# Seven block products instead of eight in parts of a gated MLP's matrix products, with the up product held the other way round

## The chip, the cores and the metric

The kernel runs on one core of one Trainium2 chip. The metric is the device time in microseconds (us) of one execution; the number given is the median of several runs. Everything is computed in float32. TensorE takes the big products in the form fp32r, so each float32 factor is cut into a rounded high part and a remainder, and a product is the sum of three: high x high, high x low and low x high.

## The reference

A trunk of two layers works on 256 tokens of width 2048. Each layer normalises, mixes the tokens (first an mLSTM, then an HGRN2 recurrence), adds the result, normalises again and runs a gated MLP with a convolution of width 3 over the tokens:

```python
def conv_glu(hn, w_up, conv_w, conv_b, w_down):
    u = hn @ w_up                       # 2048 -> 2 x 5504
    a, v = jnp.split(u, 2, axis=-1)
    ...
    for j in range(CONV_W):
        c = c + ap[:, j:j + s] * conv_w[j]
    return (jax.nn.gelu(c, approximate=False) * v) @ w_down   # 5504 -> 2048
...
    h = h + mix
    h = h + conv_glu(rmsnorm(h, norm_ffn_g[layer]), ...)
return rmsnorm(h, final_g)
```

The change is in `conv_glu` alone, in both layers.

## The kernel before

**Stream of chunks.** The program is one list of chunks that `stream` (L152) works through; each chunk is a product of all 256 tokens with a strip of weights. The strip's 16 to 22 k-tiles (128 rows of the contraction each) come from memory in pieces. `split_weights` (L122) is the generator of these pieces: a DMA on SyncE's queue brings up to 2048 columns to a tile `raw` (3 buffers), and for each 1024 of them ScalarE casts the high part `wh` (L147) and VectorE subtracts it to get the low part `wl` (L148); `wh` and `wl` have 4 buffers each. `stream` keeps 3 pieces ahead of the one that is multiplied (LOOK).

**Two forms of product.** In a chunk of kind "fm" the weights stand still in TensorE and the tokens move (L202, L209): 512 columns (high and low part of 256 tokens) pass the high weights, then 256 columns pass the low weights. The result has features on the partitions and tokens along the row. In a chunk of kind "tm" the tokens stand still and 512 columns of weights move, three matmuls for each half of the tokens (L192 to L194); the result has tokens on the partitions.

**The gated MLP** (`ffn`, L809). Its 43 feature tiles are worked through in two parts, 22 and 21. For each tile of a part there is one "fm" chunk over 16 k-tiles, with the tile's columns of a and of v as its two products. `done_up` (L820) sums the two halves of each (`fm_scaled`), multiplies by the norm's factor, applies the convolution along the row (L829 to L831), gelu and the gate, and cuts the result into high and low part: the tile `g`. Then four "tm" chunks (`project`) multiply the part's `g` tiles with 512 columns of the down weights each and add to the residual `hm` (L378).

**PSUM** has 8 banks: 4 for the chunks' sums, of which a chunk takes 2, and 4 for everything else (`aux`).

**Side work.** Small jobs (a norm's transposes, the mixers' heads) are generators in `Side`; `stream` calls `side.tick` with the modelled microseconds of each matmul, and a job whose time has come emits its next instructions. `side.until` forces jobs on until something exists, `side.drain` until none is left. On top of the order in which the program emits them, the compiler's planner orders instructions within each engine by its own estimate of when they are ready. At run time each engine takes its instructions in that order.

**Norms.** A norm's `add(c)` (L260) runs as soon as columns 512c to 512c + 511 of the residual are complete; it squares them and starts `turn` (L269), which transposes the residual's tiles (`pz`, L276) into the tiles `xt`, high and low part, for the next stage.

Of the kernel before, what the change touches and what calls it, by code (L numbers as in the profile page):

```python
# [8 lines left out]
F32 = mybir.dt.float32  # L9
# [11 lines left out]
FA = 22  # L21
FB = FT - FA
# [33 lines left out]
def trunk_kernel(ctx, tc, xT, x_d, fg_d, pp_d, cst_d, w_first, w_aq, w_ak, w_av, w_ao, w_aout,  # L56
                 w_bq, w_bv, w_bg, w_bout, w_up, w_down, out, mscr):
# [6 lines left out]
    psm = ctx.enter_context(tc.tile_pool(name="psm", bufs=4, space=PSUM))  # L64
    psa = ctx.enter_context(tc.tile_pool(name="psa", bufs=4, space=PSUM))
# [14 lines left out]

    def aux(name):
        return psa.tile([P, 512], F32, tag="aux", name=name)


    class Side:
# [3 lines left out]
        def push(self, gen):  # L89
            self.jobs.append([gen, self.now])  # L90
# [19 lines left out]
        def drain(self):  # L110
            self.until(lambda: not self.jobs)
# [9 lines left out]

    def split_weights(chunks):  # L122

        first = True
        for ch in chunks:
            total = ch.nk * ch.width
# [24 lines left out]

    def stream(chunks):  # L152
# [10 lines left out]
        for ch in chunks:  # L163
            if ch.before:
                ch.before()
            ps = [psm.tile([P, 512], F32, tag="mm", name="mm") for _ in range(3 if ch.kind == "first" else 2)]
# [49 lines left out]

    def fm_sum(ps, dst):
# [15 lines left out]
    class Norm:  # L233

        def __init__(self, gname, goff):
            self.g, self.o = gname, goff
            self.xs, self.done = [None] * KT, False

# [21 lines left out]
        def add(self, c):  # L260

            if c == 0:
                self.ss = ev.tile([P, 2, 4], F32, tag="ss8", bufs=2, name="ss8")
            cs = slice(512 * c, 512 * c + 512)
            for t in range(2):
                square(hm[:, t, cs], self.ss[:, t, c:c + 1])
            side.push(self.turn(c))

        def turn(self, c):  # L269
            yield 2.5  # L270
            for k0 in (4 * c, 4 * c + 2):
# [5 lines left out]
                for k in (k0, k0 + 1):  # L277
                    self.take(k, pz[:, (k - k0) * T:(k - k0 + 1) * T])
# [32 lines left out]
        def x(self, k):  # L311
            side.until(lambda: self.xs[k] is not None)
            return self.xs[k]

# [77 lines left out]
    def mlstm(norm, nxt):  # L392
# [204 lines left out]
        def end():  # L597
            side.drain()
            stack.close()

# [5 lines left out]
    def hgrn(norm, nxt):  # L606
# [193 lines left out]
        def end():  # L800
            side.drain()
            stack.close()

# [5 lines left out]
    def ffn(layer, norm, nxt):  # L809
        stack = ExitStack()  # L810
        box = {}
        chunks = []

        def begin():
            box["mp"] = stack.enter_context(tc.tile_pool(name="ff", bufs=1))
            box["mp"].tile([P, LEAD], F32, name="lead")
            if isinstance(nxt, FinalNorm):
                nxt.begin(box["mp"])

        def done_up(f, i, GT):  # L820
            def go(ps):
                mp, R = box["mp"], norm.R
                a = mp.tile([P, T], F32, tag="a", bufs=2, name="a")
                v = mp.tile([P, T], F32, tag="v", bufs=2, name="v")
                c = mp.tile([P, T], F32, tag="c", bufs=2, name="c")
                fm_scaled(ps[0], R, a)
                fm_scaled(ps[1], R, v)
                cw = [col("conv_w", (layer * 3 + w) * FT + f) for w in range(3)]
                dve.tensor_scalar(c, a, cw[1], col("conv_b", layer * FT + f), ALU.mult, ALU.add)  # L829
                dve.scalar_tensor_tensor(c[:, 1:T], a[:, 0:T - 1], cw[0], c[:, 1:T], ALU.mult, ALU.add)  # L830
                dve.scalar_tensor_tensor(c[:, 0:T - 1], a[:, 1:T], cw[2], c[:, 0:T - 1], ALU.mult, ALU.add)  # L831
                act.activation(c, c, AF.Gelu)
                dve.tensor_tensor(c, c, v, ALU.mult)
                g = slot(i, "g", mp)
                act.copy(g[:, 0:T], c)
                dve.tensor_tensor(g[:, T:2 * T], c, g[:, 0:T].bitcast(F32), ALU.subtract)
                GT.append(g)
            return go

        for part, (f0, nf) in enumerate(((0, FA), (FA, FB))):  # L840
            GT = []
            for i in range(nf):
                chunks.append(Chunk("fm", w_up[layer, f0 + i], KT, norm.x, done_up(f0 + i, i, GT),
                                    begin if f0 + i == 0 else None,
                                    turns=1 if part and i == 0 else 0))
            chunks += project(lambda c: w_down[layer, c][:, f0 * 512:(f0 + nf) * 512], nf,
                              lambda k, GT=GT: GT[k], nxt if part else None)
        return chunks, stack.close
# [9 lines left out]
    n0, n1, n2, n3 = Norm("mix_g", 0), Norm("ffn_g", 0), Norm("mix_g", KT), Norm("ffn_g", KT)  # L858
    nf = FinalNorm()
    chunks = mlstm(n0, n1)  # L860
    c, close0 = ffn(0, n1, n2)
    chunks += c
    c = hgrn(n2, n3)
# [7 lines left out]
    c, close1 = ffn(1, n3, nf)  # L871
    chunks += c
# [4 lines left out]
def _cols(w, width):  # L877
# [3 lines left out]
    return np.ascontiguousarray(v).reshape(N // width, P, (K // P) * width)  # L881

# [18 lines left out]
def layout(x, norm_mix_g, norm_ffn_g, mlstm_w_in, mlstm_b_gate, mlstm_head_g, mlstm_w_out, hgrn_w_in, hgrn_lb,  # L901
# [8 lines left out]
    up = A(ffn_w_up).reshape(2, KT, P, 2, FT, P).transpose(0, 4, 2, 1, 3, 5)  # L910
# [18 lines left out]
        w_up=np.ascontiguousarray(up).reshape(2, FT, P, KT * 256),  # L929
        w_down=np.stack([_cols(A(ffn_w_down)[i], 512) for i in range(2)]),  # L930
# [3 lines left out]
def build(nc, ins, out_shape=(2, P, D), **kw):  # L934
# [4 lines left out]
    with tile.TileContext(nc, schedule_with_timeline_sim=True) as tc:  # L939
        with ExitStack() as ctx:  # L940
# [3 lines left out]
                         ap["w_bout"], ap["w_up"], ap["w_down"], out, mscr, **kw)  # L944
# [12 lines left out]
```

## Time and profile before

| what | value |
|---|---|
| median of 3 runs | 2436.88 us (2436.76 to 2436.89) |
| span of the profiled execution | 2434.7 us |
| TensorE's granted clock, mean | 0.998 |
| first layer's gated MLP: up, down, up, down | 245.5, 119.7, 237.5, 117.2 us |
| second layer's: up, down, up | 245.5, 119.7, 237.5 us |
| transferred | 451.85 MB, mean 186 GB/s |

The profile shows one execution. PE is TensorE's matmuls, PEld its loads of the operand that stands still, DVE is VectorE, ACT ScalarE, POOL GpSimd. Matmuls are pipelined, so one lasts longer than the distance to the next. A group's row gives line, engine, operation, out<-in, shape and count, then after the first bar busy us and mean ns of one, and after the second bar the engine's idle time ahead of them and what ended it. Rows of a timeline give start and length in us.

### The profile page before, as it was taken

How to read it: one execution, taken by the hardware profiler on the slowest of the kernel's cores; microseconds unless marked ns; L12 is line 12 of the kernel's file. 1: busy time of each engine (PE TensorE's matmuls, PEld its weight loads, DVE VectorE, ACT ScalarE, POOL GpSimd, SP SyncE). 2: the span in 40 equal slices, each digit the busy share in tenths (PEclk: the TensorE clock that was granted, in tenths of full speed). 3: DMA queues.
4: the chain of work that ended last, by engine and by line, in shares of the span. 5: the costliest groups of instructions: out<-in, count | busy, mean ns of one | idle time of the engine just before them, and what ended most of it. 6: DMA issues, size and time to landing. Idle time of an engine off the chain costs nothing.

```text
span 2434.7 us, 36201 instructions
## 1 busy us (share of the span) xinstructions
PE 2421.4 (99%) x14319; PEld 2069.5 (85%) x14319; DVE 1691.8 (69%) x2768; ACT 1207.5 (50%) x1831; POOL 160.7 (7%) x219
## 2 busy tenths in 40 slices
PE   9999999999999999999999999999999999999998
PEld 7888888888888888888888888888888888888887
DVE  7766566777645777656888989885777754677754
ACT  6655455444434444445555555545554543444443
POOL 0100000000000000001222222220000000000000
PEclk9999999999999999999999999999999999999999
DMA  7654555555555555555445554455555555555553
GB/s 288 197 182 158 188 175 188 191 190 191 185 197 189 190 184 183 192 184 183 170 171 174 174 174 167 166 183 195 181 189 189 191 195 196 184 183 188 190 187 141
DMA packets 66202, 451.85 MB, mean 186 GB/s; under 512 B 7648, under 2 KB 8160, under 8 KB 13424
## 3 DMA queue, kind: packets, MB, share of 16 engines
q1 hardware_dynamic: 63792, 442.91, 52.6%
q0 software_dynamic: 1232, 5.31, 1.0%
q8 instruction: 112, 1.84, 0.3%
q10 hardware_dynamic: 1008, 1.32, 0.2%
q14 instruction: 58, 0.48, 0.1%
HBM read 447.35 MB, written 2.16 MB: 185 GB/s over the span
## 4 chain that ended last, share of the span: by engine, by line
PE 99%; ACT 0%; DMA 0%; issue 0%; DVE 0%; SPq 0%; POOLq 0%; POOL 0%
PE mm L202 36%; PE mm L209 18%; PE mm L192 13%; PE mm L194 13%; PE mm L193 13%; PE pn L508 1%; PE pd L694 1%; PE py L742 1%; PE pz L276 0%; PE pa L694 0%; PE S L494 0%; DMA raw<-in_w_first 0%; PE pz L763 0%; ACT xt L214 0%; PE pa L719 0%
## 5 line engine op out<-in xcount | busy, mean ns | idle before, releaser
L148 DVE TENSOR_TENSOR wl<-raw,wh 128x1024 fp32r<-128x1024 f32 (+1 forms) x848 | 1031.7, 1218 | 593.1 <-ACT wh L147 584.5
L202 PE MATMUL mm<-xt,wh 128*128 128x512 f32 x3776 | 1325.2, 396 | 0.0
L147 ACT CAST wh<-raw 128x1024 fp32r<-128x1024 f32 (+1 forms) x848 | 881.1, 1041 | 877.5 <-PE mm L194 406.0
L209 PE MATMUL mm<-xt,wl 128*128 128x256 f32 x3776 | 1057.5, 280 | 0.0
L202 PEld LDWEIGHTS mm<-xt,wh 128*128 128x128 f32 x3776 | 708.4, 188 | 165.7
L209 PEld LDWEIGHTS mm<-xt,wl 128*128 128x128 f32 x3776 | 711.7, 188 | 2.2
L194 PE MATMUL mm<-wh,g 128*128 128x512 f32 x674 | 262.8, 390 | 0.0
L192 PE MATMUL mm<-wh,g 128*128 128x512 f32 x674 | 262.6, 390 | 0.0
L193 PE MATMUL mm<-wl,g 128*128 128x512 f32 x674 | 262.3, 389 | 0.0
L192 PE MATMUL mm<-wh,xt 128*128 128x512 f32 x512 | 201.1, 396 | 2.9 <-ACT xt L214 2.2
L193 PE MATMUL mm<-wl,xt 128*128 128x512 f32 x512 | 200.6, 392 | 0.4 <-DVE wl L148 0.4
L194 PE MATMUL mm<-wh,xt 128*128 128x512 f32 x512 | 200.1, 392 | 0.0
L219 ACT COPY b<-mm 128x256 f32<-128x256 f32 x237 | 87.6, 370 | 172.5 <-PE mm L209 172.5
L194 PEld LDWEIGHTS mm<-wh,g 128*128 128x128 f32 x674 | 126.5, 188 | 26.5
L193 PEld LDWEIGHTS mm<-wl,g 128*128 128x128 f32 x674 | 126.5, 188 | 26.3
L192 PEld LDWEIGHTS mm<-wh,g 128*128 128x128 f32 x674 | 126.5, 188 | 26.0
L192 PEld LDWEIGHTS mm<-wh,xt 128*128 128x128 f32 x512 | 95.6, 188 | 23.4 <-ACT xt L214 2.9
L193 PEld LDWEIGHTS mm<-wl,xt 128*128 128x128 f32 x512 | 96.5, 188 | 19.9 <-DVE wl L148 0.8
L194 PEld LDWEIGHTS mm<-wh,xt 128*128 128x128 f32 x512 | 96.3, 188 | 19.6
L220 DVE TENSOR_TENSOR a<-mm,b 128x256 f32<-128x256 f32 x86 | 36.5, 424 | 54.2 <-ACT b L219 54.2
L686 DVE COPY kq<-QK 128x256 f32<-128x256 f32 x224 | 70.1, 335 | 0.0
L712 POOL TENSOR_TENSOR G<-G 128x384 f32<-128x384 f32 (+2 forms) x96 | 67.8, 706 | 6.3
(204 smaller groups left out, 1822.3 us busy)
## 6 DMA issues: line engine op xcount, KB each, us to landing
raw<-in_w_up SPq DMA_DIRECT2D x172, 1024.0 KB, 4.8
raw<-in_w_down SPq DMA_DIRECT2D x80, 1024.0 KB, 4.7
raw<-in_w_bq SPq DMA_DIRECT2D x48, 1024.0 KB, 4.9
raw<-in_w_ao SPq DMA_DIRECT2D x16, 1024.0 KB, 4.8
raw<-in_w_aout SPq DMA_DIRECT2D x16, 1024.0 KB, 4.7
raw<-in_w_bv SPq DMA_DIRECT2D x16, 1024.0 KB, 4.7
raw<-in_w_bg SPq DMA_DIRECT2D x16, 1024.0 KB, 4.8
raw<-in_w_bout SPq DMA_DIRECT2D x16, 1024.0 KB, 4.8
```

Source lines behind the costliest of these rows:

```text
L147: act.copy(wh[:, :m], r)
L148: dve.tensor_tensor(wl[:, :m], r, wh[:, :m].bitcast(F32), ALU.subtract)
L192: pe.matmul(ps[t], xh, wh[:, c], start=st, stop=False)
L193: pe.matmul(ps[t], xh, wl[:, c], start=False, stop=False)
L194: pe.matmul(ps[t], xl, wh[:, c], start=False, stop=sp)
L202: pe.matmul(ps[f], wh[:, c:c + P], x, start=st, stop=False)
L209: pe.matmul(ps[f][:, 0:T], wl[:, c:c + P], x[:, 0:T], start=False, stop=sp)
L219: act.copy(b, ps[:, T:2 * T])
L220: dve.tensor_tensor(dst, ps[:, 0:T], b, ALU.add)
L508: pe.matmul(pn[:, 0:258], w, v, start=(i == 0), stop=(i == len(parts) - 1))
L686: dve.tensor_copy(m[:, j].rearrange("k (m p j) -> k m p j", p=2, j=h), blocks(z, h, 0, T))
L712: pool.tensor_tensor(G2, G[:, 0:6 * n:2], G[:, 1:6 * n:2], ALU.mult)
```

## The change

**Pairs.** A new kind of chunk, `Pair`, multiplies all tokens with two strips of weights at once, b = 0 and b = 1. With the two halves of the tokens and the two k-tiles of a "couple" this is a product of 2 x 2 blocks of 128 x 128 with 128 x 512, which is eight block products, each of three matmuls. A plan has a letter for each couple: N is eight block products, S is seven (Winograd's form of Strassen's scheme), H is a single k-tile.

- In an S couple, VectorE first makes four differences of weight blocks (`T4`), which are cut into high and low parts together with three of the original blocks: 7 blocks of 512 instead of 4. The token side has four combinations as well (`forms`), made once for each couple. Three products go to sums of their own (m1, m6, m7 in banks 4 to 6), one to c22, and three straight to c11, c12 and c21.
- After the last S couple `middle` calls `combine`, which takes the four sums of m1, m6, m7 and c22 to a tile `at`; c22 then starts anew. In couples up to the last S one block of c12 is multiplied with a difference of tokens in place of the block itself.
- A `Pair` takes all four main banks. While S couples are open, `aux` has bank 7 alone.

**Up.** Four feature tiles form a group: strip b = 0 holds 512 columns of a, b = 1 of v (the eleventh group has three tiles, 384 columns). Tokens stand still now, so tokens are on the partitions. `done` evicts the four sums into `at` with the norm's factor; `raise_up`, a side job, transposes each tile's a and v (four transposes in TensorE), then does convolution, gelu, gate and the cut into `g`. The plan is NNSNSNNN.

**Down.** Parts are 16, 16 and 11 tiles. Two pairs per part, of 1024 columns each, with the plans NSNSNSNN and NSNSNH; `raise_up` makes the forms of `g`. In the second layer's last part, columns 1024 to 2047 are still two "tm" chunks.

```diff
-FA = 22
-FB = FT - FA
+PARTS = ((0, 16), (16, 16), (32, 11))
+GROUP = 4
+UP_PLAN = "NNSNSNNN"
+DOWN_PLAN = {16: "NSNSNSNN", 11: "NSNSNH"}
...
+    def split_pair(ch):
+        w, b0 = ch.w, 0
+        for kind in ch.plan:
+            n = (2 if kind == "H" else 4) * w
+            raw = wpool.tile([P, 2048], F32, tag="raw", bufs=RAW, name="raw")
+            nc.sync.dma_start(raw[:, :n], ch.src[:, b0:b0 + n])
+            b0 += n
+            if kind != "S":
+                for c0 in range(0, n, 2 * w):
+                    yield halves(raw[:, c0:c0 + 2 * w], 2 * w)
+                continue
+            T4 = ch.pool().tile([P, 2048], F32, tag="T4", bufs=1, name="T4")
+            b12 = raw[:, 0:w].unsqueeze(1).broadcast_to([P, 2, w])
+            dve.tensor_tensor(T4[:, 0:2 * w].rearrange("p (a b) -> p a b", a=2), b12,
+                              raw[:, w:3 * w].rearrange("p (a b) -> p a b", a=2), ALU.subtract)
+            dve.tensor_tensor(T4[:, 2 * w:3 * w], raw[:, 2 * w:3 * w], T4[:, 0:w], ALU.subtract)
+            dve.tensor_tensor(T4[:, 3 * w:4 * w], raw[:, 3 * w:4 * w], T4[:, 2 * w:3 * w], ALU.subtract)
+            yield halves(raw[:, w:3 * w], 2 * w)
+            yield halves(raw[:, 3 * w:4 * w], w)
+            yield halves(T4[:, 0:2 * w], 2 * w)
+            yield halves(T4[:, 2 * w:4 * w], 2 * w)
...
+                u = take()
+                product("m1", tok(k, 0), part(u, 0), fin)
+                side.tick(0.68)
+                product("c12", form(3), part(u, 1))
+                side.tick(0.68)
+                u = take()
+                product("c11", tok(k + 1, 0), part(u, 0))
+                side.tick(0.68)
+                u = take()
+                product("c22", form(0), part(u, 0), fin)
+                if fin:
+                    begun.discard("c22")
+                side.tick(0.68)
+                product("m7", form(2), part(u, 1), fin)
+                side.tick(0.68)
+                u = take()
+                product("m6", form(1), part(u, 0), fin)
+                side.tick(0.68)
+                product("c21", tok(k + 1, 1), part(u, 1))
+                if fin:
+                    ch.middle(acc)
+                    spare.banks = (7, 4, 5, 6)
...
+    def forms(x2, kind, mp, tag, fe):
...
+        if kind == "S":
+            dve.tensor_tensor(e[:, 0:P], a21, a22, ALU.add)
+            dve.tensor_tensor(e[:, P:2 * P], e[:, 0:P], a11, ALU.subtract)
+            dve.tensor_tensor(e[:, 2 * P:3 * P], a21, a11, ALU.subtract)
+            dve.tensor_tensor(e[:, 3 * P:4 * P], a12, e[:, P:2 * P], ALU.subtract)
+        else:
+            dve.tensor_tensor(e[:, 0:2 * P].rearrange("p (a b) -> p a b", a=2), x2[:, :, 0:P], x2[:, :, P:T], ALU.subtract)
+        act.copy(F[:, 0], e[:, 0:n * P])
+        dve.tensor_tensor(F[:, 1], e[:, 0:n * P], F[:, 0].bitcast(F32), ALU.subtract)
...
+        def raise_up(st):
+            while not st["ready"]:
+                yield 0.5
...
+                for n in range(2):
+                    for t in range(2):
+                        o = n * T + t * P
+                        pe.transpose(pt[:, o:o + P], at[:, t, n * 512 + j * P:n * 512 + (j + 1) * P], ident)
+                cw = [col("conv_w", (layer * 3 + k) * FT + f) for k in range(3)]
+                act.activation(c, pt[:, 0:T], AF.Identity, scale=cw[1], bias=col("conv_b", layer * FT + f))
+                dve.scalar_tensor_tensor(c[:, 1:T], pt[:, 0:T - 1], cw[0], c[:, 1:T], ALU.mult, ALU.add)
+                dve.scalar_tensor_tensor(c[:, 0:T - 1], pt[:, 1:T], cw[2], c[:, 0:T - 1], ALU.mult, ALU.add)
                 act.activation(c, c, AF.Gelu)
-                dve.tensor_tensor(c, c, v, ALU.mult)
+                dve.tensor_tensor(c, c, pt[:, T:2 * T], ALU.mult)
...
+                if i % 2 and i // 2 in st["GT"].want:
+                    st["GT"].forms[i // 2] = forms(st["GT"].c2, st["GT"].want[i // 2], mp, f"gf{i // 2}", mp)
+                yield 3.5
+            st["over"] = True
...
+        def combine(acc, at, w):
+            v5 = box["mp"].tile([P, 512], F32, tag="fe", bufs=1, name="v5")[:, 0:w]
+            s1, u4, u3, u = (at[:, t, 512 * b:512 * b + w] for t in range(2) for b in range(2))
+            act.copy(s1, acc["m1"][:, 0:w])
+            act.copy(v5, acc["c22"][:, 0:w])
+            dve.tensor_tensor(u, s1, acc["m6"][:, 0:w], ALU.add)
+            dve.tensor_tensor(u3, u, acc["m7"][:, 0:w], ALU.add)
+            dve.tensor_tensor(u4, u, v5, ALU.add)
+            dve.tensor_tensor(u, u3, v5, ALU.add)
...
+                        for n, t, b in (("c11", 0, 0), ("c12", 0, 1), ("c22", 1, 1), ("c21", 1, 0)):
+                            v = st["at"][:, t, 512 * b:512 * b + w]
+                            dve.scalar_tensor_tensor(v, acc[n][:, 0:w], norm.rc[:, t:t + 1], v, ALU.mult, ALU.add)
...
+            for c in (0, 2):
+                def middle(acc, c=c, before=before):
+                    room(before)
+                    combine(acc, before["at"], 512)
+                    for t in range(2):
+                        h = hm[:, t, 512 * c:512 * c + 1024]
+                        dve.tensor_tensor(h, h, before["at"][:, t], ALU.add)
...
+                    if part == len(PARTS) - 1:
+                        nxt.add(c)
+                        nxt.add(c + 1)
```

In a norm that feeds an up product, `turn` also makes the forms of couples 0 to 4. The weights of up and down are stored in the order in which the pairs read them.

More of the change, by code (lines that the diff above doesn't have):

```diff
@@ L110, in drain @@
         def drain(self):
-            self.until(lambda: not self.jobs)
+            self.until(lambda: all(job[2] for job in self.jobs))
     side = Side()
@@ L165, in stream, with take @@
                 ch.before()
-            ps = [psm.tile([P, 512], F32, tag="mm", name="mm") for _ in range(3 if ch.kind == "first" else 2)]
+            if ch.kind == "pair":
+                def take():
+                    fetch()
+                    return ready.pop(0)
+                stream_pair(ch, take)
+                continue
+            ps = [main.next("mm") for _ in range(3 if ch.kind == "first" else 2)]
             k = 0
@@ L313, in x, with form @@
             return self.xs[k]
+        def form(self, c):
+            side.until(lambda: c in self.forms)
+            return self.forms[c]
     class FinalNorm:
@@ L816, in begin @@
             box["mp"].tile([P, LEAD], F32, name="lead")
[L817 to L831, printed above, removed]
+            box["xf"] = tc.tile_pool(name="xf", bufs=1)
@@ new lines, in room @@
+        def room(st):
+            side.until(lambda: all("over" in o for o in st["wait"]))
+            st["at"] = box["mp"].tile([P, 2, 1024], F32, tag="at", bufs=1, name="at")
+        def combine(acc, at, w):
[7 more added lines that the diff above has]
+            dve.tensor_tensor(u, u3, v5, ALU.add)
```

236 lines of the change are left out of this document (201 added, 35 removed).

## The prediction

> **What bounds the kernel now.** I read the page first, for the busy shares and the chain of work that ended last.
>
> ```profile
> span 2434.7 us, 36201 instructions
> ...
> PE 2421.4 (99%) x14319; PEld 2069.5 (85%) x14319; DVE 1691.8 (69%) x2768; ACT 1207.5 (50%) x1831; POOL 160.7 (7%) x219
> ...
> PE 99%; ACT 0%; DMA 0%; issue 0%; DVE 0%; SPq 0%; POOLq 0%; POOL 0%
> ```
>
> TensorE is busy from end to end and makes up the whole chain; VectorE has 31% to spare on average. The second view is the busy time by stretch, cut where the line of the matmuls changes: up (L202, L209) and down (L192 to L194) of the first layer, then of the second. The last stretch also holds the kernel's end.
>
> ```profile
> core 0: us, PE busy (x) PEld busy (x) DVE busy (x) ACT busy (x) POOL busy (x), PEclk, DMA share, GB/s
> 400.65:646.17 245.52, 245.52 (x1421) 214.83 (x1420) 178.85 (x289) 123.93 (x183) 0.69 (x1) 1.00 0.56 190
> 646.17:765.88 119.71, 119.71 (x530) 99.11 (x529) 60.90 (x60) 47.53 (x48) 0.00 (x0) 1.00 0.54 192
> 765.88:1003.41 237.53, 237.53 (x1347) 206.02 (x1345) 168.07 (x266) 114.05 (x165) 0.00 (x0) 1.00 0.55 187
> 1003.41:1120.57 117.16, 117.16 (x531) 96.81 (x530) 62.55 (x71) 54.39 (x72) 0.00 (x0) 1.00 0.53 183
> 1708.57:1954.09 245.52, 245.52 (x1421) 214.74 (x1420) 178.85 (x289) 123.92 (x183) 0.71 (x1) 1.00 0.56 190
> 1954.09:2073.80 119.71, 119.71 (x531) 99.10 (x529) 60.90 (x60) 47.53 (x48) 0.00 (x0) 1.00 0.54 192
> 2073.80:2311.33 237.53, 237.53 (x1347) 206.05 (x1345) 168.07 (x266) 114.05 (x165) 0.00 (x0) 1.00 0.55 187
> ```
>
> TensorE never pauses here, at full clock, and VectorE is at 71 to 73% in up and 51 to 53% in down. So a removed matmul is worth its spacing, and VectorE's slack can be spent, until it ends last. The spacing comes from the groups of the two down stretches of the first layer.
>
> ```profile
> L192 PE MATMUL mm<-wh,g 128*128 128x512 f32 x176 | 68.5, 389 | 0.0
> L194 PE MATMUL mm<-wh,g 128*128 128x512 f32 x176 | 68.5, 389 | 0.0
> L193 PE MATMUL mm<-wl,g 128*128 128x512 f32 x176 | 68.5, 389 | 0.0
> ```
> ```profile
> L194 PE MATMUL mm<-wh,g 128*128 128x512 f32 x168 | 66.0, 393 | 0.0
> L192 PE MATMUL mm<-wh,g 128*128 128x512 f32 x168 | 65.7, 391 | 0.0
> L193 PE MATMUL mm<-wl,g 128*128 128x512 f32 x168 | 65.4, 390 | 0.0
> L276 PE MATMUL pz<-cst,hx 128*128 128x128 f32 x24 | 4.1, 272 | 0.0
> ```
>
> The first holds 528 matmuls of 512 columns in 119.71 us: 0.2267 us each, though one lasts 0.389 (they overlap). The second holds 504, worth 114.26, and 24 transposes: (117.16 - 114.26) / 24 = 0.12 us for a transpose, with the slower matmuls just behind it.
>
> **The change on TensorE.** Up takes 245.52 + 237.53 = 483.05 us a layer. After, a group of four tiles has 6 plain couples of 24 matmuls and 2 seven-product couples ("S couples") of 21: 186 matmuls, 42.17 us. Ten groups make 421.7. The eleventh is 384 columns wide; its matmul I take at 0.174, between 512 columns and the 258 of this row, by their durations: 0.2267 - (0.389 - 0.284) x 128/254.
>
> ```profile
> L508 PE MATMUL pn<-Vh,Wh 128*128 128x258 f32 x48 | 13.5, 284 | 0.0
> ```
>
> That is 32.4. Up's result now has tokens on the partitions, so each of 43 tiles needs four transposes: 172 x 0.12 = 20.6. The norm's last eight transposes stay in the stretch, 1.0. Sum 475.7, so up gains 7.3 a layer, 14.7 in all. Most of what fewer products give, 44 S couples x 3 x 0.2267 = 29.9, goes to 41.3 of transposes; the gain is left because 512-column matmuls alone are denser than the old 512 + 256 pairs (483.05 - 1.0 over 1376 pairs is 0.350; three halves of 0.2267 are 0.340). Down drops three matmuls in each of 16 + 14 S couples: 90 x 0.2267 = 20.4. TensorE's total falls by 35.1: 2399.6 by the span if nothing is late. Bounds of the transpose: 0.11 would give 3.4 more, its full duration 0.272 takes 52 back (a rival).
>
> The Trainium skill (TensorE: Matmul & The Clock Gate, Part 4) gives a transpose some 275 ns in a kernel's context. The row's 272 agrees as a duration; as a spacing the 24 above measured 0.12. With 275 the 344 would cost 94.6, not 41.3.
>
> **The change on VectorE.** These rows price it and the work around it.
>
> ```profile
> L148 DVE TENSOR_TENSOR wl<-raw,wh 128x1024 fp32r<-128x1024 f32 x824 | 1013.5, 1231 | 576.1 <-ACT wh L147 567.4
> L147 ACT CAST wh<-raw 128x1024 fp32r<-128x1024 f32 x824 | 865.0, 1051 | 857.2 <-PE mm L194 388.2 <-issue 241.4 <-PE mm L202 206.3
> L831 DVE SCALAR_TENSOR_TENSOR c<-a,pp,c 128x255 f32<-128x255 f32 x86 | 41.0, 477 | 0.0
> L836 DVE TENSOR_TENSOR g<-c,g 128x256 fp32r<-128x256 f32 x86 | 35.9, 418 | 0.0
> L378 DVE TENSOR_TENSOR hx<-hx,mm 128x512 f32<-128x512 f32 x46 | 30.0, 681 | 8.5 <-PE mm L194 8.5
> L335 DVE TENSOR_TENSOR hx<-hx,fg 128x512 f32<-128x512 f32 x6 | 3.9, 684 | 0.0
> L781 DVE SCALAR_TENSOR_TENSOR sg<-mm,rc,sg 128x512 f32<-128x512 f32 x8 | 5.9, 742 | 0.0
> L496 DVE TENSOR_TENSOR W<-W,S 128x128 f32<-128x128 f32 x16 | 3.8, 278 | 0.0
> L364 ACT ACTIVATE jk<-hx 128x512 f32<-128x512 f32 x32 | 20.1, 629 | 8.2 <-DVE hx L347 6.9 <-DVE hx L378 1.0 <-DVE t L620 0.2
> L214 ACT ACTIVATE xt<-pz,pp 128x256 fp32r<-128x256 f32 x48 | 21.0, 473 | 20.9 <-PE pz L276 14.0 <-DVE xt L215 6.9
> L215 DVE SCALAR_TENSOR_TENSOR xt<-pz,pp,xt 128x256 fp32r<-128x256 f32 x48 | 21.7, 479 | 8.2 <-ACT xt L214 8.0
> ```
>
> In a dense stretch consecutive instructions overlap:
>
> ```profile
> 1421.71 0.43 DVE L707 TENSOR_TENSOR QK<-QK,G 128x256 f32<-128x256 f32 x1
> 1422.05 2.35 DVE L148 TENSOR_TENSOR wl<-raw,wh 128x1024 fp32r<-128x1024 f32 x2
> 1424.32 0.49 DVE L686 COPY kq<-QK 128x256 f32<-128x256 f32 x2
> ```
>
> Start to start: 1.135 for 1024 columns, 0.34 for 256, hence 0.60 for 512 and 0.20 for 128, about 0.08 to 0.1 under the durations. A plain couple needs 2 x 1.135 = 2.27 us. An S couple needs its four differences (1.135 + 2 x 0.60, and 0.25 because they follow one another) and 3 x 1.135 + 0.60 of splitting: 6.6, while TensorE spends 21 x 0.2267 = 4.8. Per up group: weights 6 x 2.27 + 2 x 6.6 = 26.8; four evictions in done at 0.66, 2.6; four sums in combine, 2.4; four tiles of raise_up at 2 x 0.39 + 2 x 0.34, 5.8; forms of two couples (0.7 plain; 4 x 0.20 + 0.60 for S), 2.1. Together 39.7 against TensorE's 42.17 + 16 x 0.12 = 44.1: 90%. A down pair of 16: 5 x 2.27 + 3 x 6.6 + 2.4 + 2 x 1.135 + 2.4 = 38.2 against (5 x 24 + 3 x 21) x 0.2267 = 41.5: 92%. ScalarE has 38 casts of 512 columns at 1.05 / 2 in a group, 20 us, and smaller work; it is no bound.
>
> On the average VectorE fits; in places it does not. Piece n+3 is split while piece n is multiplied, so little runs ahead. From the start of a group that follows another, TensorE comes to the last piece of the second S couple after 108 matmuls and 16 transposes, 24.5 + 1.9 = 26.4 us. By then VectorE owes: the evictions 2.6, raise_up 5.8, forms 2.1, one plain piece 1.1, S 6.6, plain 2.27, S 6.6 = 27.1 us. So **0.7 late**; by full durations (2.97 + 7.14 + 2.64 + 1.23 + 6.98 + 2.46 + 6.98) 30.4, **4.0 late**; with the first S couple's differences put into the quiet tail of the group before, 2 us early. There are 16 such groups: 11, 64 or 0 us. Besides, an S couple's last piece has its buffer only 15 matmuls, 3.4 us, before it is used, and cast 1.05, subtraction 1.23 and one such instruction in front take 3.5: 0.1 in each of 74, 7 us at most. I take **15 us** of 0 to 71, near the low price because wide instructions were seen to overlap, and the planner puts weights first: VectorE was full for 15 us here, and TensorE did not wait.
>
> ```profile
> 1280.00:1295.00 15.00, 15.00 (x68) 12.43 (x67) 15.00 (x29) 7.44 (x11) 8.28 (x10) 1.00 0.55 195
> ```
>
> There the other work could wait, though; S pieces can't.
>
> The skill has a rule against me (VectorE: DVE Perf Modes, Terms): after every operation the pipe drains, and the next cannot issue until it is empty. By that the durations add up and the sum is the 4.0 a group. The trace disagrees: two of 1.23 took 2.27 from start to next start.
>
> **Small waits.** A pair holds all four main banks, so the next pair's c21 waits for an eviction queued behind up to three others; it has nine matmuls, 2.0 us, of cover, and after it c21's products and all behind them on TensorE would wait: 0 to 1 us, within the 15. At the first layer's end, columns 1024 to 2047 arrive at once; evictions 2.4, four squares at 0.63 and a transposed tile (0.27 + 0.47 + 0.48, some 1.5 with the steps between) make 6.4 against 16 old pairs, 5.6, before k = 8: 1 us, once. Weight transfers keep their bytes and count (56% busy).
>
> Sum: 2434.7 - 35.1 + 15 + 1 = 2415.6 by the span; the runs' median lies 2.2 above it (2436.88): **2418 us**.
>
> **Rivals.** *Nothing is late*: the planner moves the differences into the tails. For it speaks the 90%; the time is 2402 (2399 to 2410). *VectorE ends last at the second S couple* (the other side): 4 us late in 16 groups, and by the same count 1.6 in six first down pairs, 74 us, so 2402 + 74 = 2476. It decides from where VectorE's 27.1 becomes 28.5, 5% above my spacings: from there 2.1 x 16 + 1 eats the 35. For it: only three pieces run ahead, and VectorE does its queue in order; against: the full 15 us above. *In between*: 25 to 40 us of waits, 2432 to 2442, no visible difference. *Transposes don't overlap*: each waits for the one before to leave; 344 x 0.152 = 52 more, 2454; the 24 in down speak against it. *Denser matmuls aren't had* behind transposes: up breaks even, 2433, the upper edge of mine.
>
> **How the numbers follow.** My case, 2410 to 2432: 0.41; nothing late: 0.25; in between: 0.09; VectorE last: 0.21; transposes: 0.04. A measurement tells 0.2%, 4.9 us, from no change: faster 0.66, same 0.09, slower 0.25. The range leaves out the first rival's lower edge and the worst of VectorE: 2398 to 2466. Of the likeliest alone it is 2410 to 2432.
>
> **What would show it.** Up stretches of about 476 us plus waits; idle of TensorE before matmuls with the weight low halves, released by the subtraction, at the second S couple of groups 2 to 4; VectorE at 85 to 95% in up and down; transposes at 0.12. I am wrong if TensorE waits at every S couple, or for banks, or if its busy time fell by much less than 35.

## The result and the profile after

The changed kernel takes **2511.15 us** (2509.06 to 2514.16) against 2436.89: ratio 1.0305, interval 1.029 to 1.0319. The forecast was 2418 with a range to 2466; the kernel is 74 us slower instead of 19 faster. First the page of the changed kernel: span, busy times, chain of waits.

```profile
span 2510.9 us, 34534 instructions
...
PE 2434.8 (97%) x13159; PEld 2021.6 (81%) x13159; DVE 2033.5 (81%) x3115; ACT 1401.9 (56%) x2114; POOL 160.3 (6%) x219
...
PE 75%; DVE 17%; issue 4%; ACT 3%; DMA 2%; POOLq 0%; POOL 0%; ACTq 0%; DVEq 0%
```

TensorE ran 1160 matmuls fewer, but was busy 13 us longer, and idle for 76 us of the span instead of 13. The chain now has 17% of VectorE, where it had none. Busy time by stretch says where; the columns are those of the prediction's second fence.

```profile
400.82:581.04 180.22, 178.47 (x806) 144.55 (x804) 154.33 (x216) 111.84 (x156) 0.69 (x1) 1.00 0.50 181
581.04:670.61 89.57, 85.83 (x383) 69.80 (x382) 80.85 (x97) 49.82 (x61) 0.00 (x0) 1.00 0.54 198
670.61:850.20 179.59, 177.15 (x793) 143.42 (x793) 153.89 (x208) 106.09 (x145) 0.00 (x0) 1.00 0.50 183
850.20:939.11 88.91, 85.80 (x383) 69.81 (x382) 80.77 (x97) 49.37 (x61) 0.00 (x0) 1.00 0.54 197
939.11:1063.83 124.72, 121.97 (x591) 105.05 (x591) 105.47 (x149) 73.72 (x106) 0.00 (x0) 1.00 0.51 178
1063.83:1139.90 76.07, 65.22 (x282) 51.28 (x281) 63.37 (x83) 41.05 (x61) 0.00 (x0) 0.96 0.47 169
1139.90:1772.29 632.39, 607.64 (x4748) 517.07 (x4749) 498.19 (x983) 315.56 (x570) 139.40 (x177) 0.97 0.46 161
```

The rows are up and down, three times, and the HGRN mixer behind the first layer. The mixer isn't touched by the change, and yet it grew by 44.4 us; here it is in the kernel before:

```profile
1120.57:1708.57 588.00, 588.00 (x4742) 504.28 (x4741) 487.08 (x962) 309.32 (x548) 139.88 (x178) 1.00 0.51 175
```

The same stretches of the kernel e5 below, which has seven products in the up groups alone and hardly waits, give a measured time without waits for all but the down pairs:

```profile
401.00:577.03 176.03, 176.03 (x806) 145.33 (x805) 146.78 (x193) 108.85 (x150) 0.69 (x1) 1.00 0.55 191
577.00:666.00 89.00, 89.00 (x401) 73.55 (x400) 50.97 (x58) 37.89 (x45) 0.00 (x0) 1.00 0.56 189
666.00:840.60 174.60, 174.60 (x793) 144.12 (x792) 145.42 (x184) 104.79 (x141) 0.00 (x0) 1.00 0.56 193
929.60:1050.20 120.60, 120.60 (x591) 105.11 (x590) 99.46 (x134) 72.50 (x103) 0.00 (x0) 1.00 0.56 189
1050.20:1113.40 63.20, 63.20 (x294) 52.17 (x293) 40.58 (x61) 35.15 (x52) 0.00 (x0) 1.00 0.55 189
1113.40:1703.10 589.70, 589.49 (x4750) 505.11 (x4750) 493.31 (x975) 314.98 (x567) 139.69 (x177) 1.00 0.51 172
```

With the 90 matmuls that seven products save in down taken off (20.4 us), e5's span of 2423.7 makes 2403.3; the changed kernel took 107.6 more. By stretches, over both layers:

| part | changed | without waits (from e5) | difference |
|---|---|---|---|
| HGRN mixer | 632.4 | 589.7 | 42.7 |
| down, six stretches | 473.8 | 450.7 - 20.4 = 430.3 | 43.5 |
| up, six stretches | 963.2 | 943.5 | 19.7 |
| rest | | | 1.7 |

**The mixer.** A head's first product pa needs VectorE's QK. These are TensorE's and VectorE's rows of one head in the kernel before, by start and length:

```profile
1232.47 0.96 DVE L707 TENSOR_TENSOR QK<-QK,G 128x256 f32<-128x256 f32 x2
...
1233.27 0.39 PE L718 MATMUL pa<-QK 128*128 128x128 f32 x2
...
1234.42 0.89 PE L694 MATMUL pd<-kq 128*32 128x32 f32 x78
```

and of the same head after:

```profile
1255.37 0.45 PE L869 MATMUL pd<-kq 128*32 128x32 f32 x28
...
1258.54 0.95 DVE L882 TENSOR_TENSOR QK<-QK,G 128x256 f32<-128x256 f32 x2
...
1259.10 0.77 PE L893 MATMUL pa<-QK 128*128 128x128 f32 x2 [3.29 <-DVE QK L882]
```

Now 28 matmuls of the product pd stand ahead of pa, and the whole group comes earlier than QK is ready. TensorE waits 3.29 us with no projection in between. The granted clock (third column from the right) falls too, in stretches around this wait:

```profile
1248.40:1255.40 7.00, 7.00 (x36) 5.52 (x35) 7.00 (x11) 3.78 (x5) 6.60 (x6) 1.00 0.44 150
1255.40:1259.10 3.70, 0.41 (x30) 0.33 (x29) 3.70 (x9) 0.00 (x0) 2.76 (x5) 0.92 0.66 208
1259.10:1264.00 4.90, 4.90 (x92) 4.21 (x93) 4.33 (x14) 0.80 (x2) 0.00 (x0) 0.50 0.54 181
```

In seven of the 16 heads 28 to 72 matmuls of pd stand ahead of pa, and TensorE waits 3.3 to 3.9 us; in the other nine none does, and it waits 0.1 us at most. The waits view of the changed kernel (total, times, longest) has the seven first:

```profile
PE pa L893 <- DVE QK L882: 24.6, 7, 3.9
PE c L215 <- DVE hx L1105: 11.5, 7, 5.7
```

Some 25 us are waits; the rest of the 43 is work at half clock (the mixer's row above has a mean granted clock of 0.97).

**The end of a down pair** is the largest single wait in the table's second row. VectorE and TensorE at the seam of the first layer's last part:

```profile
1096.80 1.23 DVE L1100 TENSOR_TENSOR hx<-hx,at 128x1024 f32<-128x1024 f32 x1
1097.93 1.22 DVE L182 TENSOR_TENSOR wl<-raw,wh 128x1024 fp32r<-128x1024 f32 x1
...
1100.27 1.23 DVE L1100 TENSOR_TENSOR hx<-hx,at 128x1024 f32<-128x1024 f32 x1
1101.40 1.29 DVE L1105 TENSOR_TENSOR hx<-hx,c 128x512 f32<-128x512 f32 x2
...
1102.24 0.77 PE L215 MATMUL c<-wh,g 128*128 128x512 f32 x1 [5.72 <-DVE hx L1105]
```

The next pair's first matmul needs the bank that the first eviction (L1105) frees. Ahead of this eviction VectorE works off the sums of `combine`, the next pair's splits, and two adds (L1100) of 1.23 us, whose results no matmul is waiting for. TensorE waits 5.72 us and goes on at half clock.

### The profile page after: what moved, and what is told of

The parts are those of the page before. It is cut to its first block, busy times and chain, and to the rows that moved or that the text cites. A ratio compares the mean times of both kernels' runs of the same rounds, so it can differ in the third digit from the quotient of the medians.

```text
span 2510.9 us, 34534 instructions
## 1 busy us (share of the span) xinstructions
PE 2434.8 (97%) x13159; PEld 2021.6 (81%) x13159; DVE 2033.5 (81%) x3115; ACT 1401.9 (56%) x2114; POOL 160.3 (6%) x219
## 4 chain that ended last, share of the span: by engine, by line
PE 75%; DVE 17%; issue 4%; ACT 3%; DMA 2%; POOLq 0%; POOL 0%; ACTq 0%; DVEq 0%
PE c L215 33%; PE mm L336 9%; PE mm L326 6%; DVE wl L182 6%; PE mm L327 6%; PE mm L328 6%; PE m L215 4%; PE mm L343 4%; DVE wl L174 2%; ACT wh L181 2%; PE pt L1017 1%; DVE QK L881 1%; DMA raw<-in_w_down 1%; DVE kq L861 1%; DVE T L198 1%
## 5 line engine op out<-in xcount | busy, mean ns | idle before, releaser
L215 PE MATMUL c<-wh,xt 128*128 128x512 f32 (+1 forms) x2024 | 664.9, 389 | 6.9 <-DVE hx L1105 2.7
L182 DVE TENSOR_TENSOR wl<-raw,wh 128x1024 fp32r<-128x1024 f32 (+3 forms) x513 | 570.2, 1130 | 77.6 <-ACT wh L181 76.3
L181 ACT CAST wh<-raw 128x1024 fp32r<-128x1024 f32 (+3 forms) x513 | 485.0, 974 | 215.5 <-PE c L215 170.4
L174 DVE TENSOR_TENSOR wl<-raw,wh 128x1024 fp32r<-128x1024 f32 (+1 forms) x340 | 414.8, 1222 | 190.3 <-ACT wh L173 189.1
L173 ACT CAST wh<-raw 128x1024 fp32r<-128x1024 f32 (+1 forms) x340 | 350.0, 1032 | 294.9 <-PE mm L328 150.3
L215 PEld LDWEIGHTS c<-wh,xt 128*128 128x128 f32 x2024 | 378.6, 188 | 86.7 <-issue 7.4
L215 PE MATMUL c<-wl,xt 128*128 128x512 f32 (+1 forms) x1012 | 390.6, 387 | 2.7 <-DVE wl L182 2.5
L336 PE MATMUL mm<-xt,wh 128*128 128x512 f32 x1024 | 362.0, 397 | 2.6 <-DVE hx L1105 2.6
L215 PE MATMUL c<-wh,g 128*128 128x512 f32 x808 | 279.7, 400 | 16.1 <-DVE hx L1105 8.8
L343 PE MATMUL mm<-xt,wl 128*128 128x256 f32 x1024 | 289.1, 283 | 0.0
L215 PE MATMUL c<-wh,F 128*128 128x512 f32 (+1 forms) x680 | 250.6, 392 | 0.0
L181 ACT CAST wh<-T 128x1024 fp32r<-128x1024 f32 (+1 forms) x148 | 153.5, 1039 | 166.9 <-PE c L215 147.9
L182 DVE TENSOR_TENSOR wl<-T,wh 128x1024 fp32r<-128x1024 f32 (+1 forms) x148 | 178.7, 1210 | 64.7 <-ACT wh L181 63.5
L336 PEld LDWEIGHTS mm<-xt,wh 128*128 128x128 f32 x1024 | 191.8, 188 | 45.2 <-issue 3.0
L215 PEld LDWEIGHTS c<-wl,xt 128*128 128x128 f32 x1012 | 190.3, 188 | 40.2 <-DVE wl L182 6.0
L215 PEld LDWEIGHTS c<-wh,g 128*128 128x128 f32 x808 | 152.8, 190 | 53.8 <-issue 6.1
L343 PEld LDWEIGHTS mm<-xt,wl 128*128 128x128 f32 x1024 | 193.4, 189 | 2.2 <-DVE wl L174 0.4
L215 PE MATMUL c<-wl,g 128*128 128x512 f32 x404 | 159.6, 395 | 3.3 <-DVE wl L182 3.3
L215 PEld LDWEIGHTS c<-wh,F 128*128 128x128 f32 x680 | 128.8, 190 | 25.1 <-issue 0.2
```

The source lines that it names most:

```text
L173: act.copy(wh[:, :m], r)
L174: dve.tensor_tensor(wl[:, :m], r, wh[:, :m].bitcast(F32), ALU.subtract)
L181: act.copy(wh[:, :m], r)
L182: dve.tensor_tensor(wl[:, :m], r, wh[:, :m].bitcast(F32), ALU.subtract)
L215: pe.matmul(acc[name][:, 0:w], a, b, start=name not in begun, stop=sp and i == 2)
L336: pe.matmul(ps[f], wh[:, c:c + P], x, start=st, stop=False)
```

## The experiments

The first theory had two causes: the banks' new names move the mixer's instructions, and VectorE's work at the seams of the MLP keeps TensorE waiting. Its rivals: the mixer grows since the MLP leaves work behind, and VectorE is late inside the groups, by its load. In kernels with pools L206 is the product's line (L215 after the change), L172 and L173 are the cast and the subtraction of a pair's weights (L181, L182), L1074 the evictions of `done` in up (L1085), and L1094 or L1091 the evictions at a down pair's end (L1105).

**e1: the kernel before, with the change's bank names alone**

```diff
-            ps = [psm.tile([P, 512], F32, tag="mm", name="mm") for _ in range(3 if ch.kind == "first" else 2)]
+            ps = [main.next("mm") for _ in range(3 if ch.kind == "first" else 2)]
...
-        return psa.tile([P, 512], F32, tag="aux", name=name)
+        return spare.next(name)
```

> The kernel before, with one thing of the change: the eight PSUM banks as eight tiles of fixed names taken in turn, instead of two pools of four buffers each. Theory 'banks': the fixed turn makes the planner put a head's products earlier among TensorE's matmuls in the HGRN stage, where they wait for VectorE; the stage grows from 588 to about 632 us as in the changed kernel, the time to 2481 us (2470 to 2492), the gated MLP stays as it was. Rival 'left behind': the HGRN stage loses 44 us because of the state in which the changed MLP leaves queues and buffers; then this kernel takes 2437 us.

2477.73 us, ratio 1.017 (1.0153 to 1.0187). The waits view and TensorE's timeline of this kernel:

```profile
PE pa L730 <- DVE QK L719: 23.9, 7, 3.6
```
```profile
1234.40 0.45 PE L706 MATMUL pd<-kq 128*32 128x32 f32 x28
1238.14 0.77 PE L730 MATMUL pa<-QK 128*128 128x128 f32 x2 [3.29 <-DVE QK L719]
```

The same seven waits and the same order, without any of the change's arithmetic; up and down kept 245.5, 119.7, 237.5 and 117.2 us. A bank named by its number, in place of the next free one of a pool, is enough.

**e2: the changed kernel with two pools of four banks**

```diff
-        acc = {n: main.next(n) for n in ("c11", "c12", "c22", "c21")}
+        acc = {n: mm(n) for n in ("c11", "c12", "c22", "c21")}
...
-                    spare.banks = (7,)
-                    acc.update(m1=bank(4, "m1"), m6=bank(5, "m6"), m7=bank(6, "m7"))
+                    acc.update(m1=aux("m1"), m6=aux("m6"), m7=aux("m7"))
```

> The changed kernel with the banks back in two pools of four buffers each (the three extra sums taken from the second pool). Theory 'banks': the HGRN stage is back at 588 us and the time at 2511 - 44 = 2467 us (2458 to 2476); the MLP's waits of some 66 us stay. Rival 'left behind': 2511 us.

2467.92 us (1.0113 to 1.0143 of before); the mixer takes 591.8 us. So 43 us are the banks' names; by its span (2468.1) some 65 over 2403.3 are left. All kernels below have pools.

**e3: all couples plain**

```diff
-UP_PLAN = "NNSNSNNN"
-DOWN_PLAN = {16: "NSNSNSNN", 11: "NSNSNH"}
+UP_PLAN = "NNNNNNNN"
+DOWN_PLAN = {16: "NNNNNNNN", 11: "NNNNNH"}
```

> As the one before, but every couple plain: no seven-product couple, no differences, no forms, no sums in combine. TensorE gets 74 x 3 matmuls more, 50 us: 2399.6 + 50.3 + 2.2 = 2452 us if nothing is late. Theory 'VectorE': the waits in the MLP come from the work of the seven-product couples, so nothing is late here: 2450 to 2462 us, and slower than before all the same, by the transposes. Rival 'one set of banks': the pair's four banks, all needed by the next pair, cause the waits; then they stay, some 45 us, and the time is 2490 to 2515 us. Rival 'dear transposes': up stretches longer than 24 matmuls x 8 couples x 0.2267 + 16 x 0.12 = 45.4 us a group by several us.

2453.12 us (1.0051 to 1.0081), without waits: up 181.37, 179.96, 124.12, down 89.01, 89.01, 63.21. Seven products with all that they bring made the kernel 15 us slower (2467.9), though they take 50 us of matmuls away. The edit spares VectorE one thing more: without an S couple `done` evicts an up group on ScalarE.

**e4: the four differences on GpSimd**

```diff
-            dve.tensor_tensor(T4[:, 0:2 * w].rearrange("p (a b) -> p a b", a=2), b12,
+            pool.tensor_tensor(T4[:, 0:2 * w].rearrange("p (a b) -> p a b", a=2), b12,
```

(and the two below it in the same way)

> The changed kernel with pooled banks, and the weight differences of a seven-product couple made on GpSimd, which is idle in the MLP, instead of VectorE: 2.6 us less of VectorE for each of 74 couples. Theory 'VectorE': the waits fall by half or more, 2467 to some 2425 to 2445 us. Rival 'one set of banks': 2467 us. Third: GpSimd needs 0.8 to 1.3 us for 256 columns here, so 6.5 to 10 us for a couple's 2048, and seven-product couples follow one another every 10.2 us: if it takes the 10, its results come late and the time is over 2467 us.

2510.86 us: slower than e2 by 43, which tells nothing of VectorE's load, since the edit slowed VectorE itself. Groups of e2, then of e4, with mean ns behind the comma:

```profile
L173 DVE TENSOR_TENSOR wl<-raw,wh 128x1024 fp32r<-128x1024 f32 x411 | 493.2, 1218 | 79.2 <-ACT wh L172 77.8
...
L189 DVE TENSOR_TENSOR T<-raw 128x1024 f32<-128x1024 f32 x70 | 85.3, 1218 | 7.3 <-DMA raw<-in_w_down 6.8 <-DMA raw<-in_w_up 0.2
```
```profile
L173 DVE TENSOR_TENSOR wl<-raw,wh 128x1024 fp32r<-128x1024 f32 x411 | 629.4, 1552 | 87.3 <-ACT wh L172 85.6
```
```profile
L189 POOL TENSOR_TENSOR T<-raw 128x1024 f32<-128x1024 f32 x70 | 206.4, 2948 | 1021.2 <-DVE wl L173 443.1 <-DMA raw<-in_w_up 390.1 <-DMA raw<-in_w_down 163.6
```

VectorE was spared 85 us for the wide differences and some 96 for the narrow ones, but L173 alone took 136 us more. GpSimd is slower at the differences, so the pieces come later. The experiment is inconclusive on VectorE's load; that had to be tested by plans.

**e5 and e6: seven products in up alone, in down alone**

```diff
-DOWN_PLAN = {16: "NSNSNSNN", 11: "NSNSNH"}
+DOWN_PLAN = {16: "NNNNNNNN", 11: "NNNNNH"}
```

(e6 has this plan as it was, and UP_PLAN "NNNNNNNN")

> Pooled banks, seven-product couples in up alone (NNSNSNNN), down all plain. Against the all-plain kernel's 2453 us TensorE has 44 x 3 matmuls less, 29.9 us: 2423 us without waits. Theory 'VectorE late inside a group': the up stretches of the changed kernel were 22 us over, so 2445 us (2438 to 2452), with TensorE's waits on the subtraction or the cast at the second seven-product couple. Rival 'the pair's end in down': the waits belong to the sums, the adds to the residual and the four banks at the end of a down pair; then up alone has few, 2423 to 2432 us.

> Pooled banks, up all plain, seven-product couples in down alone (NSNSNSNN, NSNSNH). TensorE has 30 x 3 matmuls less than all-plain, 20.4 us: 2433 us without waits. If down makes its own waits ('the pair's end in down'), the 45 us that the down stretches of the changed kernel were over come back: 2470 to 2480 us, with waits for the adds to the residual at the start of the next pair. If they were carried over from up's backlog on VectorE, few are left: 2433 to 2442 us.

e5: **2425.52 us**, 0.9953 (0.994 to 0.9967), faster than both kernels, as the rival had it. e6: 2463.79 us (1.0096 to 1.0124), between its two forecasts. In up, 27.6 us are gained on e3, nearly all that the matmuls are worth; in down 20.4 us of matmuls turn into a loss of 10.7. e6's waits view:

```profile
PE c L206 <- DVE hx L1094: 11.7, 5, 5.6
PE mm L315 <- DVE hx L1094: 3.2, 1, 3.2
```

Both are for the evictions at a pair's end, and so is a third one of 2.6 us. Up in e6, where the forms of `g` are made but no couple has seven products, takes 181.37, 179.96 and 124.13 us, just as without forms.

**e7 and e8: the couples spread out, and one for each pair**

```diff
-UP_PLAN = "NNSNSNNN"
-DOWN_PLAN = {16: "NSNSNSNN", 11: "NSNSNH"}
+UP_PLAN = "NNSNNSNN"
+DOWN_PLAN = {16: "NSNNSNNN", 11: "NSNNNH"}
```

(e8: "NNSNNNNN", "NSNNNNNN", "NSNNNH")

> Pooled banks, two seven-product couples a pair and further apart: up NNSNNSNN, down NSNNSNNN and NSNNNH; 63 couples instead of 74. TensorE has 42.8 us less than all-plain: 2410 us without waits. Theory 'bursts': with two plain couples between, VectorE owes 29.4 us against 31.8 of TensorE at the second one's last piece, 2.4 early, and in down three plain couples follow the last one; waits fall below 15 us: 2410 to 2425 us, faster than both kernels. Rival 'load': VectorE has nearly as much to do on the whole, and the waits stay at 40 us or more: over 2450 us.

> Pooled banks, one seven-product couple a pair: up NNSNNNNN, down NSNNNNNN and NSNNNH; 33 couples. TensorE has 22.4 us less than all-plain: 2430.7 us without waits. Theory 'bursts': next to no waits, 2431 to 2437 us. Rival 'a fixed price for each pair that has such couples' (the four sums and the adds at its end, whatever their number): the waits stay near half of those of the changed kernel, 2455 to 2465 us.

2435.65 us (0.9989 to 1.0006) and 2440.04 us (1.0003 to 1.0021); both lie between their theory and their rival. Spreading helps against e2 (178.5 us for the first up stretch instead of 179.6, down 87.7 instead of 91.1, where e7 also has one couple fewer a pair), but e7, with 57 matmuls fewer than e5 (12.9 us), is some 23 us above what these make, and e8 with about half the couples some 9. Less load per pair gives shorter waits; it doesn't say whether load or order is at fault.

**e9: e6 with the adds behind the evictions**

```diff
                     combine(acc, before["at"], 512)
-                    for t in range(2):
-                        h = hm[:, t, 512 * c:512 * c + 1024]
-                        dve.tensor_tensor(h, h, before["at"][:, t], ALU.add)
...
                         dve.tensor_tensor(h, h, acc[n], ALU.add)
+                    for t in range(2):
+                        h = hm[:, t, 512 * c:512 * c + 1024]
+                        dve.tensor_tensor(h, h, before["at"][:, t], ALU.add)
```

> The kernel with seven block products in the down pairs only (2463.8 us), with one change of order: the two 1024-wide adds of the previous part sum to the residual (L1100), which at a pair's end stand on VectorE ahead of the four evictions that free the banks, are moved behind these four. VectorE's work stays the same to the instruction. Theory 'the banks' order': TensorE waited there 15 us behind these evictions (11.7 us on the banks c and 3.2 us on mm in the waits of that kernel) and ran at half clock after each wait; with the evictions some 2.4 us earlier most of it goes: 2440 to 2452. Rival 'the load': what is late is VectorE's sum over a pair's end and the next pair's start, whatever its order: 2460 to 2467, the waits then stand at the next pair's operands instead of its banks.

2443.15 us (1.0016 to 1.0038), 20.6 us less than e6 with the same instructions. VectorE at the seam that cost 5.72 us, and the waits view:

```profile
1089.05 0.69 DVE L1046 TENSOR_TENSOR at<-at,v 128x512 f32<-128x512 f32 x1
1089.65 0.69 DVE L1091 TENSOR_TENSOR hx<-hx,c 128x512 f32<-128x512 f32 x1
1090.25 1.23 DVE L173 TENSOR_TENSOR wl<-raw,wh 128x1024 fp32r<-128x1024 f32 x1
1091.38 1.89 DVE L1091 TENSOR_TENSOR hx<-hx,c 128x512 f32<-128x512 f32 x3
```
```profile
PE c L206 <- DVE hx L1091: 1.0, 1, 1.0
```

The first eviction follows the last sum of `combine` at once. The wait for banks went from 11.7 to 1.0 us, and that part from 73.6 to 64.8. The banks' order is the larger cause in down; some 10 of e6's 31 us stay.

**e10 and e11: more on top of e5**

```diff
-UP_PLAN = "NNSNSNNN"
+UP_PLAN = "NNSNSNSN"
```

(e10; e11 has e5's up plan, "NNSNSNNN" and "NSNNNH" for the second pair of each down part alone, and e9's order)

> Seven block products in three of the eight couples of an up group instead of two, none in the down pairs, tiles in two pools of four banks (with two couples: 2425.5 us). TensorE's sum falls by 22 couples x 3 matmuls x 0.2267 = 15.0 us, to about 2410. VectorE's work of an up group grows to some 42 us of 43.4. Theory 'below TensorE's time it stays hidden': 2409 to 2414. Rival 'the last couples of a group are late': the seventh couple's operands and the combination fall into the same last fifth of the group, each of the 22 groups waits 1 to 2 us: 2425 to 2450.

> Seven block products in two of eight couples of the up groups as before, and in the second pair of each down part alone (the first pair plain), with the adds of the part sum behind the evictions; two pools of four banks. Against the kernel with the up groups alone (2425.5 us) TensorE's sum falls by 9 couples x 3 matmuls x 0.2267 = 6.1 us. Theory 'a pair's end costs more than its couples save': each of the five or six pairs' ends gives back 2 to 4 us and the time is 2428 to 2440. Rival 'a plain pair behind or ahead gives VectorE the room': no waits, 2418 to 2421.

e10: 2473.38 us (1.0135 to 1.0163), worse than even the rival said. 15 us of matmuls fewer, 48 us more. Its waits view:

```profile
PE c L206 <- DVE at L1074: 14.9, 22, 1.3
PE c L206 <- DVE wl L173: 7.6, 18, 0.6
PE c L206 <- ACT wh L172: 5.4, 18, 0.9
```

One wait in each of the 22 groups is for the evictions of `done` (L1074): with an S couple in place seven, `combine` comes with one couple left, and its sums stand on VectorE just ahead of these evictions. The others are for pieces of weights, and nearly as long together. Of the 63 us lost these rows hold 28; most of the rest lies in gaps between matmuls too short to count as idle. So the release of the banks costs time in up as well, once the load reaches the group's end; what each of the two would cost alone wasn't tried.

e11: 2425.65 us (0.994 to 0.9965), level with e5; both theories miss. Parts 1 and 2 of down take 87.66 us, 1.36 less than plain, which is all six matmuls. But up takes 176.87, 175.45 and 121.53, some 0.8 more in each of six stretches, where the forms of `g` for these couples are now made.

**e12: the changed kernel with pools and with e9's order**

> The changed kernel, all its couples of seven block products kept, with the two things that the other runs named mended together: two pools of four banks in place of fixed names (2467.9 us with that alone) and the adds of the part sum behind the four evictions at a pair's end (worth 20.7 us where the down pairs alone have seven products). Without waits it would take about 2403 us: the all-plain kernel's 2453.1 less the 50.3 us of matmuls that the seven products save; so 65 us of the 2467.9 are waits. Theory 'the pair's end is the same whatever the up groups do': 2467.9 - 20.7 = 2447, within 2443 to 2451. Rival 'the up groups' load comes on top at the seams': with the evictions earlier the next group's operands are still late, 2455 to 2466. Rival 'the up groups had been late behind the pair's end': the seams heal altogether, 2405 to 2425.

2439.44 us (1.0001 to 1.0019), better by 28.5 than e2, and just outside the first theory's bounds: down 86.6 us four times (90 to 91 in e2), the last part of the first layer 67.2 (73.7). What its span (2436.9) has left over 2403.3 stands in up, 179.19, 179.07 and 123.38 us against e5's 176.03, 174.60 and 120.60, some 19 us over both layers, and in some 14 us of down. So the order gave nothing back in up, which is nearly as long as in e2 and in the changed kernel.

## Why the prediction was wrong, point by point

**TensorE's sum: right.** e5's gated MLP of the first layer takes 712.5 us; the prediction's 475.7 for up and 236.9 for plain down are 712.6. The split is another (up 471.2, down 241.2), since 44 of up's transposes run in the down stretches. Transposes at 0.12 us, 512 columns at 0.2267 and 384 at 0.174 hold. e3 and e5 differ by 27.6 us where the matmuls came to 29.9, four of the 44 couples being narrower. The rivals that transposes don't overlap and that denser matmuls aren't had fall.

**VectorE in an up group: right in place, and near in size there.** The ledger said 0.7 us late at matmul 108 of a later group, 11 us in all, 15 with small things. This is TensorE in the third group, whose first matmul starts at 488.98:

```profile
515.28 0.78 PE L215 MATMUL m<-wh,F 128*128 128x512 f32 x2
515.90 0.40 PE L215 MATMUL c<-wh,xt 128*128 128x512 f32 x1
516.51 0.72 PE L215 MATMUL c<-wh,xt 128*128 128x512 f32 x2 [0.21 <-ACT wh L181]
```

The second gap is 0.61 us instead of 0.23, 110 matmuls into the group, and the neighbours are stretched by 0.1 each: 0.7 together. It ends with a cast, not with the subtraction that the prediction named: ahead of this cast ScalarE had that of the differences, and VectorE made the last difference at 513.69 only, behind an instruction of the forms (L365) and one of `raise_up`. By the spacings of TensorE's matmuls ten of the 16 later groups lose 0.6 to 1.6 us at this place, some 9 together. The rest of up's 19.7 us stands elsewhere, such as behind the evictions at a group's start and behind a down pair's. The ledger's term of 2.1 us for the forms of `g` is the one that tips it: without forms (e5, 25.0 us owed of 26.4) nothing waits, forms without S couples (e6) cost nothing, both together do, and e11, with forms for fewer couples, lost 0.8 a stretch. That it is VectorE's share of the forms, and not ScalarE's casts for them, is argued from the ledger. The rival with 4 us a group falls.

**"Small waits: a pair holds all four main banks ... 0 to 1 us, within the 15" failed.** Down lost 43.5 us, and TensorE waited there for banks, which the prediction had named as a sign that it is wrong. The step looked at the evictions alone, queued behind up to three others. It left out what stands ahead of all four on VectorE at a pair's end: the sums of `combine`, the next pair's splits, and the two adds that the change had put there. The ledger had been made to the second S couple only, and for down only as an average, 38.2 of 41.5 us. e9 shows that the order of two adds is worth 20.6 us, e12 28.5 with up's seven products beside it, 26 of them in down. With the same plan down takes 458 us in e6 and 471 in e2: S couples in up make it dearer, which fits one engine that carries a debt across the seam; which instructions carry it wasn't traced. With the adds behind, 10 us in e9 and 14 in e12 stay in down; their cause is open.

**A term was missing: the banks' names.** The prediction counted four main and four spare banks as before, so the mixer had no place in its sum. It cost 41 us in e1 and gave 43 back in e2, more than the whole gain forecast: the naming alone does it and undoes it. Why the planner puts pd ahead of pa when banks have names wasn't tried; that its estimate of when a bank is ready differs is only argued.

So the chance of 0.25 for "slower" stood on the wrong mechanism, and the number 2476 of its rival "VectorE ends last" lies nearer to the result than the forecast only by accident.

## What to carry to other kernels

A change that renames or re-pools buffers can reorder code it doesn't touch: compare the instruction order of the stages it leaves alone, and give them a term in the sum. Where an engine works off a queue at a seam, write down what stands ahead of the one instruction that frees a bank, and put work that nobody waits for behind it. Take saved matmuls only in stretches where the helping engine's ledger to the last release of the stretch, not its average, stays below TensorE's time: here two of eight couples in up (e5, 2425.5 us) paid, a third did not.

## What the hardware showed unexpectedly

**The length of a wait doesn't tell alone whether the clock halves.** Behind the idle time of 3.29 us the granted clock is 0.50 in the stretch shown above, and matmuls of 512 columns stand 0.43 us apart until 1265.1, 6 us on. The two rows are from there:

```profile
1263.40 0.63 PE L328 MATMUL mm<-wh,xt 128*128 128x512 f32 x1
1263.83 0.63 PE L326 MATMUL mm<-wh,xt 128*128 128x512 f32 x1
```

The wait of 5.72 us has the same behind it, one of 2.59 us at the mixer's start has not; by stretch, from the mixer's start and from the end of the 5.72:

```profile
1139.90:1144.00 4.10, 4.10 (x24) 3.64 (x25) 3.13 (x7) 1.82 (x5) 0.00 (x0) 1.00 0.67 222
...
1102.24:1106.00 3.76, 3.76 (x10) 2.98 (x11) 2.25 (x4) 2.00 (x6) 0.00 (x0) 0.50 0.46 144
```

But there is no edge between these lengths. In e12 a wait of 2.27 us has the spacing of 0.43 us behind it:

```profile
1089.86 0.61 PE L206 MATMUL c<-wh,g 128*128 128x512 f32 x1 [2.27 <-DVE hx L1091]
1090.26 0.63 PE L206 MATMUL c<-wl,g 128*128 128x512 f32 x1
1090.69 1.05 PE L206 MATMUL c<-wh,g 128*128 128x512 f32 x2
```

In the changed kernel the clock is also 0.50 from 1999.22 to 2002.63, behind a wait of 1.68 us, while in e4 a wait of 3.46 us (until 2464.85) has a clock of 1.00 behind it. The trace's clock is at half for 3.41 or 6.83 us at a time, and the two such stretches from 1258.52 and 1395.06 begin 40 times 3.41 us apart. That fits a decision taken at fixed steps of 3.41 us, for which it matters how a wait falls on them; this wasn't tested. The Trainium skill (TensorE: Matmul & The Clock Gate, HAM oscillation — how this bites in real kernels) warns of idle gaps above some 3.4 us; the traces here don't bear that out as an edge, with halving behind 1.68 us and none behind 3.46.

**GpSimd's subtractions slow VectorE's.** In e4 VectorE's subtraction of two operands in SBUF (L173, of `raw`) took 1552 ns on average instead of 1218; one of them took 3.42 us from 657.13 on, beside a wide difference on GpSimd (656.15, 3.32 us). GpSimd needed 2948 ns for what VectorE does in 1218; whether it would be faster beside an idle VectorE isn't shown. The Trainium skill (SBUF — State Buffer, Who interferes with whom) says that a VectorE instruction with two SBUF inputs contends with a GpSimd instruction that reads SBUF; the trace agrees.
